# RMS norm with SiLU on one core: VectorE's and ScalarE's code aligned to instruction-fetch blocks

## The chip, the cores and the metric

The kernel runs on 1 core of a Trainium2 chip. The metric is the device time of one execution in microseconds; the kernel before takes 316.89 us (median of 3 runs, 316.89 to 317.03). TensorE is PE in the profile, VectorE DVE, ScalarE ACT, GpSimd POOL and SyncE SP; a small q behind a name means the engine's sequencer, which issues DMAs and waits on semaphores.

## The reference

For an input x of 8 x 1024 rows with 2048 float32 numbers each, a vector gamma of 2048 numbers and eps = 1e-5:

```python
rms = np.sqrt(np.mean(x ** 2, axis=-1, keepdims=True) + eps)
out = gamma * x / rms
return out * (1 / (1 + np.exp(-out)))
```

64 MB are read and 64 MB are written.

## The kernel before

The 8192 rows are cut into 16 blocks of 512 rows. A block has 128 partitions with J = 4 rows each, 4 MB in all. On the chip a ring of BUFS = 6 blocks holds them; block b lies in place b modulo 6. Each block is loaded, worked on in place and stored from the same place, so the load of block b + 6 waits until the store of block b is complete. Blocks 4 and 5 are a pair: each partition holds 8 rows that follow each other in memory, and one transfer loads both (`load_pair`, L69 to L71).

The steps of a block, with their lines:

- `load` (L66, L67): one DMA of 4 MB, issued by ScalarE's queue.
- `squares_scalar` (L78) and `squares_vector` (L86): the sums of squares of the block's four rows, one or two of them on ScalarE and the rest on VectorE, each with its read of the accumulator.
- `root` (L95): ScalarE takes the square root, with a table load ahead of it. `invert` (L100): VectorE takes the reciprocal.
- `multiply` (L105): VectorE multiplies each row by its factor and by g, which is gamma on all partitions.
- `silu` (L113): ScalarE applies Silu, two rows at a time, with a table load ahead of it. `store` (L117): one DMA of 4 MB, issued by SyncE.

The last block takes another way: VectorE multiplies by g alone (L177), and ScalarE's Silu (L179) takes the factor as its scale.

The order of the work is written out by hand under `tc.manual_schedule()`: the instructions of an engine stand in its queue as the code names them. The first ones are what the change touches:

- L121: ScalarE issues the load of block 0.
- L122, L123: VectorE fills `ones` and `eps_t`.
- L124: ScalarE runs one small Square on `ones`, which brings a table load ahead of it.
- L125: SyncE issues the load of gamma (8 KB) into one partition of g. L126 to L128: TensorE multiplies it by a row of ones, so that gamma comes to stand on all partitions of the PSUM tile `junk_v`.
- L129: ScalarE issues the load of block 1.
- L130: VectorE copies `junk_v` to g. L131: ScalarE copies one column of `junk_v`.
- L132 to L135: ScalarE issues the loads of blocks 2 and 3, and of the pair of blocks 4 and 5.

After that comes the loop over the blocks. The load of block 6 stands in ScalarE's queue ahead of the squares of block 3's turn, and the later ones between a block's squares (`loads`) or between the two Silu steps (`between`).

In the built program VectorE has 170 instructions in the kernel's body and ScalarE 145, the waits that stand alone among them.

Of the kernel before, what the change touches and what calls it, by code (L numbers as in the profile page):

```python
# [1 line left out]

# [4 lines left out]

ACT = mybir.ActivationFunctionType
ALU = mybir.AluOpType


@with_exitstack
def kernel(
    ctx: ExitStack,
    tc: tile.TileContext,
    x: bass.AP,
    gamma: bass.AP,
    eps: bass.AP,
    out: bass.AP,
):  # L20

    nc = tc.nc
    P = nc.NUM_PARTITIONS
    f32 = mybir.dt.float32
    x2 = x.flatten_outer_dims()
    o2 = out.flatten_outer_dims()  # L30
    n, d = x2.shape
    J = 4
    BUFS = 6
    nblk = n // (P * J)
    PAIRS = (4,)

    def view(t, b):

        for q in PAIRS:
            if b in (q, q + 1):  # L40
                both = t[q * P * J:(q + 2) * P * J, :].rearrange("(p j) d -> p (j d)", p=P, j=2 * J)
                return both[:, (b - q) * J * d:(b - q + 1) * J * d]
        return t[b * P * J:(b + 1) * P * J, :].rearrange("(p j) d -> p (j d)", p=P, j=J)

    singles = ctx.enter_context(tc.tile_pool(name="singles", bufs=1))
    small = ctx.enter_context(tc.tile_pool(name="small", bufs=2))
    psum = ctx.enter_context(tc.tile_pool(name="psum", bufs=1, space=bass.MemoryType.PSUM))

    Q = 4
    w = d // Q  # L50
    g = singles.tile([P, d], f32)
    eps_t = singles.tile([P, 1], f32)
    ones = singles.tile([P, P], f32)
    junk_a = psum.tile([P, d], f32, name="junk_a")
    junk_v = psum.tile([P, d], f32, name="junk_v")
    ring = singles.tile([P, BUFS * J * d], f32, name="xt")
    sss, rmss, rstds = {}, {}, {}

    def rows(b, j, k):
        at = (b % BUFS) * J + j  # L60
        return ring[:, at * d:(at + k) * d]

    def row(b, j):
        return rows(b, j, 1)

    def load(b):  # L66
        nc.scalar.dma_start(out=rows(b, 0, J), in_=view(x2, b))  # L67

    def load_pair(b):  # L69
        both = x2[b * P * J:(b + 2) * P * J, :].rearrange("(p j) d -> p (j d)", p=P, j=2 * J)  # L70
        nc.scalar.dma_start(out=rows(b, 0, 2 * J), in_=both)  # L71

    def squares_scalar(b, loads=()):


        sss[b] = small.tile([P, J], f32, name="ss")
        for j in range(share(b)):
            nc.scalar.activation(out=junk_a, in_=row(b, j), func=ACT.Square,  # L78
                                 accum_out=sss[b][:, j:j + 1])
            if j == 0:  # L80
                for s in loads:
                    load(s)

    def squares_vector(b):
        for j in range(share(b), J):
            nc.vector.tensor_tensor_reduce(  # L86
                out=junk_v, in0=row(b, j), in1=row(b, j), scale=1.0, scalar=0.0,
                op0=ALU.mult, op1=ALU.add, accum_out=sss[b][:, j:j + 1])

    def share(b):  # L90
        return 1 if 4 <= b <= 12 and b % 2 == 0 else 2

    def root(b):
        rms = small.tile([P, J], f32, name="rms")
        nc.scalar.activation(out=rms, in_=sss.pop(b), func=ACT.Sqrt, scale=1.0 / d, bias=eps_t)  # L95
        rmss[b] = rms

    def invert(b):
        rstd = small.tile([P, J], f32, name="rstd")
        nc.vector.reciprocal(out=rstd, in_=rmss.pop(b))  # L100
        rstds[b] = rstd

    def multiply(b):
        for j in range(J):
            nc.vector.scalar_tensor_tensor(out=row(b, j), in0=row(b, j), scalar=rstds[b][:, j:j + 1],  # L105
                                           in1=g, op0=ALU.mult, op1=ALU.mult)

    def silu(b, between=()):
        for h in range(0, J, 2):
            if h:  # L110
                for s in between:
                    load(s)
            nc.scalar.activation(out=rows(b, h, 2), in_=rows(b, h, 2), func=ACT.Silu)  # L113
        store(b)

    def store(b):
        nc.sync.dma_start(out=view(o2, b), in_=rows(b, 0, J))  # L117

    with tc.manual_schedule():

        load(0)  # L121
        nc.vector.memset(ones, 1.0)  # L122
        nc.vector.memset(eps_t, float(eps))  # L123
        nc.scalar.activation(out=junk_a[:, 0:1], in_=ones[:, 0:1], func=ACT.Square)  # L124
        nc.sync.dma_start(out=g[0:1, :], in_=bass.AP(tensor=gamma.tensor, offset=gamma.offset, ap=[[d, 1], [1, d]]))  # L125
        for c in range(Q):  # L126
            cols = slice(c * w, (c + 1) * w)
            nc.tensor.matmul(junk_v[:, cols], ones[0:1, :], g[0:1, cols], start=True, stop=True)  # L128
        load(1)  # L129
        nc.vector.tensor_copy(out=g, in_=junk_v)  # L130
        nc.scalar.copy(out=junk_a[:, 0:1], in_=junk_v[:, d - 1:d])  # L131
        for b in range(2, PAIRS[0]):  # L132
            load(b)
        for b in PAIRS:
            load_pair(b)  # L135

        last = nblk - 1
        SOON = 3  # L140
        squares_scalar(0)
        squares_vector(0)
        root(0)
        invert(0)
        for b in range(last):
            loads = [b + 3] if BUFS + 2 <= b + 3 < nblk else []
            between = []
            if b + 3 == BUFS:

                load(BUFS)  # L150
                between = [BUFS + 1]
            if b < SOON:
                multiply(b)
                squares_scalar(b + 1, loads)
                silu(b)
                squares_vector(b + 1)
                root(b + 1)
            elif b < last - 1:
                squares_scalar(b + 1, loads)
                squares_vector(b + 1)  # L160
                root(b + 1)
                multiply(b)
                silu(b, between)
            else:
                multiply(b)
                squares_scalar(b + 1)
                silu(b)
                squares_vector(b + 1)
                root(b + 1)
            if b + 1 < last:  # L170
                invert(b + 1)


        for j in range(J):
            if j == J // 2:
                invert(last)
            nc.vector.tensor_mul(out=row(last, j), in0=row(last, j), in1=g)  # L177
        for j in range(J):
            nc.scalar.activation(out=row(last, j), in_=row(last, j), func=ACT.Silu,  # L179
                                 scale=rstds[last][:, j:j + 1])  # L180
        store(last)


# [1 line left out]
_INS = ['x', 'gamma', 'eps']  # L185
_OUTS = [((8, 1024, 2048), 'float32')]

_NUMBERS = {'eps': 9.999999747378752e-06}


# [26 lines left out]
```

## Time and profile before

| What | Value |
| --- | --- |
| median of 3 runs | 316.89 us (316.89 to 317.03) |
| the profiled execution's span, first to last instruction | 315.4 us |
| last instruction of ScalarE's Silu (L179) ends | 291.5 us |
| VectorE busy | 235.2 us |
| ScalarE busy | 212.5 us |
| PE busy | 7.2 us |
| HBM read, written | 67.12 MB, 67.11 MB |
| longest wait in total: VectorE's L86 for loads | 25.9 us in 8 waits |

Times count from the span's start. The page has the busy time of each engine, the span in 40 equal slices (a digit is the busy share in tenths), and the DMA queues: q1 carries the stores and gamma, q10 the loads, q14 instructions. A line of a queue gives packets, MB and the share of 16 DMA engines' time. The DMA view of a window counts the packets that start in it.

The start in order of time, from the timeline:

| Start, us | What |
| --- | --- |
| 0.73 | ScalarE's queue issues the load of block 0, SyncE's that of gamma |
| 0.83 | VectorE, first memset (L122), 0.17 us |
| 1.13 | ScalarE, table load of L124, 1.28 us |
| 1.20 | ScalarE's queue issues the load of block 1 |
| 2.43 | ScalarE, L124 |
| 3.10 | TensorE, first weight load (L128) |
| 10.32 | VectorE, copy of g (L130), 2.29 us |
| 12.71 | ScalarE, L131 |
| 12.73 | ScalarE's queue issues the loads of blocks 2 and 3, at 13.58 that of the pair |
| 13.19 | VectorE, first sum of squares (L86) |
| 35.29 | SyncE's queue issues the first store |

### The profile page before, as it was taken

How to read it: one execution, taken by the hardware profiler on the slowest of the kernel's cores; microseconds unless marked ns; L12 is line 12 of the kernel's file. 1: busy time of each engine (PE TensorE's matmuls, PEld its weight loads, DVE VectorE, ACT ScalarE, POOL GpSimd, SP SyncE). 2: the span in 40 equal slices, each digit the busy share in tenths (PEclk: the TensorE clock that was granted, in tenths of full speed). 3: DMA queues.
4: the chain of work that ended last, by engine and by line, in shares of the span. 5: the costliest groups of instructions: out<-in, count | busy, mean ns of one | idle time of the engine just before them, and what ended most of it. 6: DMA issues, size and time to landing. Idle time of an engine off the chain costs nothing.

```text
span 315.4 us, 436 instructions
## 1 busy us (share of the span) xinstructions
PE 7.2 (2%) x8; PEld 2.5 (1%) x8; DVE 235.2 (75%) x157; ACT 212.5 (67%) x137; POOL 0.2 (0%) x4
## 2 busy tenths in 40 slices
PE   6300000000000000000000000000000000000000
PEld 2000000000000000000000000000000000000000
DVE  0679697944999999999693996939969399994000
ACT  1269998952289968993919849097591999999000
POOL 0000000000000000000000000000000000000000
DMA  8999999999999999999999999999999999999996
GB/s 333 411 453 411 386 532 399 399 440 424 428 437 424 437 432 432 432 432 440 424 440 424 445 420 457 407 457 407 465 399 465 399 465 399 465 403 461 411 453 270
DMA packets 4468, 134.24 MB, mean 426 GB/s; under 512 B 497, under 2 KB 497, under 8 KB 497
## 3 DMA queue, kind: packets, MB, share of 16 engines
q10 hardware_dynamic: 2160, 67.11, 49.6%
q1 hardware_dynamic: 2306, 67.12, 49.3%
q14 instruction: 2, 0.02, 0.0%
HBM read 67.12 MB, written 67.11 MB: 426 GB/s over the span
## 4 chain that ended last, share of the span: by engine, by line
DMA 55%; ACT 18%; DVE 14%; issue 2%; another core or an unknown queue 2%; ACTq 1%; DVEq 0%
DMA out_dram<-xt 40%; DMA xt<-in_x_dram 15%; ACT xt L113 9%; DVE xt L105 9%; DVE junk_v L86 5%; ACT junk_a L78 3%; ACT L95 2%; ACT xt L179 2%; ACT L113 1%; ACTq L212 1%; ACT rms L95 1%; ACTq L67 0%; ACT L179 0%; DVE rstd L100 0%
## 5 line engine op out<-in xcount | busy, mean ns | idle before, releaser
L105 DVE SCALAR_TENSOR_TENSOR xt<-xt,rstd,g 128x2048 f32<-128x2048 f32 x60 | 137.0, 2346 | 0.1
L113 ACT ACTIVATE xt<-xt 128x4096 f32<-128x4096 f32 x30 | 107.3, 3610 | 7.4 <-DVE xt L105 7.3
L86 DVE CUSTOM_DVE_ANT_0 junk_v<-xt 128x2048 f32<-128x2048 f32 x37 | 85.0, 2296 | 26.6 <-DMA xt<-in_x_dram 25.9
L78 ACT ACTIVATE junk_a<-xt 128x2048 f32<-128x2048 f32 x27 | 50.6, 1873 | 34.5 <-DMA out_dram<-xt 22.7
L95 ACT ACT_TABLE_LOAD x15 | 19.2, 1283 | 20.1 <-DMA out_dram<-xt 10.9
L113 ACT ACT_TABLE_LOAD x14 | 18.0, 1283 | 0.2
L100 DVE RECIPROCAL rstd<-rms 128x4 f32<-128x4 f32 x16 | 2.8, 174 | 15.0 <-ACT rms L95 15.0
L130 DVE COPY g<-junk_v 128x2048 f32<-128x2048 f32 x1 | 2.3, 2291 | 9.3 <-PE junk_v L128 9.3
L177 DVE TENSOR_TENSOR xt<-xt,g 128x2048 f32<-128x2048 f32 x4 | 8.9, 2278 | 0.0
L95 ACT ACTIVATE rms<-ss,eps_t 128x4 f32<-128x4 f32 x16 | 4.8, 297 | 5.5 <-DVE ss L86 5.3
L179 ACT ACTIVATE xt<-xt,rstd 128x2048 f32<-128x2048 f32 x4 | 7.7, 1990 | 0.0
L128 PE MATMUL junk_v<-g,ones 1*128 1x512 f32 x8 | 7.2, 1072 | 3.1 <-DMA g<-in_gamma_dram 3.1
L131 ACT COPY junk_a<-junk_v 128x1 f32<-128x1 f32 x1 | 0.1, 144 | 10.1 <-DVE g L130 10.1
L86 DVE DVE_READ_ACCUMULATOR2_ANT ss<- 128x1 f32 x37 | 5.2, 141 | 0.0
L78 ACT ACTIVATION_READ_ACCUMULATOR junk_a<-xt 128x1 f32 x27 | 5.0, 186 | 0.0
L128 PEld LDWEIGHTS junk_v<-g,ones 1*128 1x128 f32 x8 | 2.5, 325 | 6.2 <-issue 6.2
L124 ACT ACT_TABLE_LOAD x1 | 1.3, 1283 | 1.1 <-PEq L198 1.1
L179 ACT ACT_TABLE_LOAD x1 | 1.3, 1283 | 0.0
L122 DVE MEMSET ones<- 128x128 f32 x1 | 0.2, 165 | 0.8 <-PEq L198 0.8
L124 ACT ACTIVATE junk_a<-ones 128x1 f32<-128x1 f32 x1 | 0.2, 174 | 0.0
L198 POOL MEMSET const-bfloat16-1.0<- 128x1 bf16 x1 | 0.1, 103 | 0.0
L198 POOL MEMSET const-uint8-127<- 128x1 uint8 x1 | 0.1, 103 | 0.0
(3 smaller groups left out, 0.3 us busy)
## 6 DMA issues: line engine op xcount, KB each, us to landing
out_dram<-xt SPq DMA_DIRECT2D x16, 4096.0 KB, 39.1
xt<-in_x_dram ACTq DMA_DIRECT2D x14, 4096.0 KB, 26.6
g<-in_gamma_dram SPq DMA_DIRECT2D x1, 8.0 KB
xt<-in_x_dram ACTq DMA_DIRECT2D x1, 61.8
```

Source lines behind the costliest of these rows:

```text
L78: nc.scalar.activation(out=junk_a, in_=row(b, j), func=ACT.Square, accum_out=sss[b][:, j:j + 1])
L86: nc.vector.tensor_tensor_reduce(out=junk_v, in0=row(b, j), in1=row(b, j), scale=1.0, scalar=0.0, op0=ALU.mult, op1=ALU.add, accum_out=sss ...
L95: nc.scalar.activation(out=rms, in_=sss.pop(b), func=ACT.Sqrt, scale=1.0 / d, bias=eps_t)
L100: nc.vector.reciprocal(out=rstd, in_=rmss.pop(b))
L105: nc.vector.scalar_tensor_tensor(out=row(b, j), in0=row(b, j), scalar=rstds[b][:, j:j + 1], in1=g, op0=ALU.mult, op1=ALU.mult)
L113: nc.scalar.activation(out=rows(b, h, 2), in_=rows(b, h, 2), func=ACT.Silu)
L124: nc.scalar.activation(out=junk_a[:, 0:1], in_=ones[:, 0:1], func=ACT.Square)
L128: nc.tensor.matmul(junk_v[:, cols], ones[0:1, :], g[0:1, cols], start=True, stop=True)
L130: nc.vector.tensor_copy(out=g, in_=junk_v)
L177: nc.vector.tensor_mul(out=row(last, j), in0=row(last, j), in1=g)
L179: nc.scalar.activation(out=row(last, j), in_=row(last, j), func=ACT.Silu, scale=rstds[last][:, j:j + 1])
L212: with _tile.TileContext(nc) as tc:
```

## The change

Two lines are added that are no work. `addr_align(FETCH, max_nops=0)` tells the program's loader that the next instruction of this engine begins at a multiple of FETCH instructions (256 in the built program) of the engine's code in memory. The instructions in between are filling; with `max_nops=0` a branch jumps over them, so they are not run. On VectorE the directive stands ahead of its first instruction of the kernel (L122), on ScalarE behind the issue of block 1's load (L129) and ahead of L131. No other instruction is added, removed or moved. Three lines are added in all, so lines behind them have a number higher by 1 to 3 in the kernel after.

```diff
     J = 4
     BUFS = 6
+    FETCH = bass.FETCH_BLOCK_INSTRUCTIONS
     nblk = n // (P * J)
...
         load(0)
+        nc.vector.addr_align(FETCH, max_nops=0)
         nc.vector.memset(ones, 1.0)
         nc.vector.memset(eps_t, float(eps))
         nc.scalar.activation(out=junk_a[:, 0:1], in_=ones[:, 0:1], func=ACT.Square)
...
         load(1)
+        nc.scalar.addr_align(FETCH, max_nops=0)
         nc.vector.tensor_copy(out=g, in_=junk_v)
         nc.scalar.copy(out=junk_a[:, 0:1], in_=junk_v[:, d - 1:d])
```

## The prediction

> **What bounds the kernel now.** I read the page's slices and queue list first, then the chain that ended last, then the DMA view in narrow windows, and last the packet records of the trace one by one.
>
> ```profile
> span 315.4 us, 436 instructions
> DMA  8999999999999999999999999999999999999996
> DMA packets 4468, 134.24 MB, mean 426 GB/s; under 512 B 497, under 2 KB 497, under 8 KB 497
> q10 hardware_dynamic: 2160, 67.11, 49.6%
> q1 hardware_dynamic: 2306, 67.12, 49.3%
> q14 instruction: 2, 0.02, 0.0%
> DMA 55%; ACT 18%; DVE 14%; issue 2%; another core or an unknown queue 2%; ACTq 1%; DVEq 0%
> ```
>
> The DMA row is at nine or more in 38 of 40 slices, while VectorE is busy for 75% of the span and ScalarE for 67%. Loads (q10) and stores (q1) together take 98.9% of what 16 DMA engines have. So the DMA engines set the time. An engine of computation that is some us late costs nothing as long as transfers stay queued. The third queue line is the one that this change can touch: two packets that carry instructions.
>
> The windows of the DMA view tell when they run.
>
> ```profile
> DMA packets 15, 0.47 MB, mean 778 GB/s; under 512 B 0, under 2 KB 0, under 8 KB 0
> q14 instruction: 1, 0.01, 3.2%
> ```
>
> That is 92.5 to 93.1 us; the window from 106.4 to 107 us shows the other one:
>
> ```profile
> DMA packets 7, 0.11 MB, mean 178 GB/s; under 512 B 3, under 2 KB 3, under 8 KB 3
> q14 instruction: 1, 0.01, 3.2%
> ```
>
> Both lie where the DMA engines are full. The packet records give start, duration, bytes and queue, but no DMA engine. I joined each packet to the one that starts within some ns of its end. This gives 16 chains, one for each DMA engine, and each holds 240 packets of 32 KB at 1.213 us and 8 of 64 KB. No chain has a gap above 0.05 us between 2.9 us and its end: all 16 are never idle. Fifteen chains end between 312.91 and 313.39 us, and one at 314.28 us. The window from 313.39 to 314.29 us holds only that chain's last, small packet:
>
> ```profile
> DMA packets 1, 0.00 MB, mean 0 GB/s; under 512 B 1, under 2 KB 1, under 8 KB 1
> ```
>
> The last store is complete when the slowest DMA engine is, so this one chain sets the end by 0.89 us. It is the chain that carries the instruction packet of 106.49 us. There the instruction packet took 0.309 us and the 32 KB packet after it 1.747 us in place of 1.213: 0.309 + 0.534 = 0.84 us. The packet of 92.71 us, on another chain, took 0.309 us and its successor 1.333: 0.309 + 0.120 = 0.43 us; that chain ends at 313.39. Without its fetch the late chain would end at 314.28 - 0.84 = 313.44, beside the others.
>
> Who fetches is not recorded. The packets start 1.05 and 1.11 us after VectorE starts a sum of squares (91.66 and 105.38 us), and ScalarE starts a Silu at 91.69 us. By then the built program stands at about the 50th to the 60th instruction on each of the two. So I take it that VectorE and ScalarE each cross an edge of their code there, one packet of 8 KB each.
>
> **The change, part by part.** It adds one directive on each of the two engines and removes nothing. The built programs show nothing moved: the same order of work on every engine, with 170 instructions and one directive on VectorE, 145 and one on ScalarE. The directive's alignment is 256 instructions, so either engine's remaining code is shorter than one aligned block.
>
> *VectorE's branch, ahead of the memset of L122.* The trace shows no branch of this kind. Its cost lies between a semaphore instruction (17 to 28 ns) and a fetch from memory, for which the nearest row is gamma's 8 KB load: issued at 0.73 us, used by TensorE at 3.13 us, so 2.4 us. Behind the branch stands the memset (0.83 us). For it wait ScalarE's L124 with the second load issue (1.20 us) behind it, and TensorE's weight load (3.10 us, beside gamma's landing). At 2.4 us the memset ends at about 3.4 us, TensorE is 0.3 us late, and so are the copy of g (10.32 us) and the issues of loads 2 to 5 (12.73 us). These must be in the queue before loads 0 and 1 are through: the second load ends at 22.77 us, and the first load's packets start up to 2.2 us after their issue. So 22.77 - 2.2 - 12.73 = 7.8 us are free. The second load itself, at 3.6 us instead of 1.2, is due by about 1.64 + 8 x 1.21 - 2.2 = 9.1 us. Cost: nothing, for anything between the two ends. Its packet falls at about 1 us, before the first data packet (1.64 us): nothing again.
>
> *ScalarE's branch, behind the second load issue.* Behind it stand L131 and the loads from 12.73 us on. ScalarE waits 10.1 us before L131 for the copy of g anyway, so a stall of 2.4 us plus two packets ahead of it (2 x 1.21) is hidden. Its fetch, however, starts at about 1.6 us plus a latency like the 1.05 us above, when the chains are just filling: first packets start between 1.64 and 2.88 us and take up to 2.39 us. One DMA engine pays between nothing (if the packet slips in ahead of that engine's first data) and 0.84 us, the dearest of the two above. I take 0.43, the nearer row, as part of it falls into the ragged start. Fifteen of the chains, without fetches, would end at 312.91 to 313.39, mean 313.17; 313.17 + 0.43 = 313.60, and 313.44 is the floor that the once late chain sets.
>
> *What goes away.* Neither engine crosses an edge in the full stretch, so 0.84 and 0.43 us leave two chains. Late next is the chain of the new ScalarE fetch, at 313.44 to 313.9, likeliest 313.6 to 313.7.
>
> **Sum.** 313.64 - 314.28 = -0.64 us. The profiled span is 315.43 us and the median of the runs 316.89, which is 1.46 us above; I keep that distance. 316.89 - 0.64 = **316.25 us**, 0.20% below. A difference of 0.2% (0.63 us) is about what a measurement of this kernel can tell from no change, and the forecast lies on that line.
>
> The Trainium skill ("Runtime: NRT & Kernel Launch", Instruction fetch mechanics) says that crossing a block edge costs one bump of a queue's tail and is mostly hidden. For the two engines' own time this agrees: no idle time of theirs is charged to a fetch. By that rule nothing would be won and the time would stay at 316.89, which is the fourth case below. The trace speaks against it at the DMA engines: 0.84 us on the one chain that ends last.
>
> **The rivals.**
>
> *More fetches than before, stacked on one DMA engine (slower).* A jump leaves the sequence of the code, so its target may have to be fetched, and the block behind it too. Two fetches of ScalarE on one DMA engine at the start, when all are filling, cost 2 x 0.43 to 2 x 0.84. On the chain with the least slack that ends at 313.44 + 0.86 = 314.30 to 313.44 + 1.69 = 315.13, so 316.9 to 317.7 us. It decides once two packets share a DMA engine that has less than 0.84 us of slack. For it: the gap of 13.8 us between the two packets of before lets each belong to one engine, so engines may have a DMA engine of their own. Against: the part behind the branch may be in the engine already.
>
> The same section of the Trainium skill warns that a taken branch out of the two fetched blocks must wait for a transfer. No row here shows such a branch.
>
> *The edges come back.* If the edge that counts lies every 128 instructions (8 KB, what one instruction packet carries: the built program gives 64 bytes for an instruction), both engines cross another one behind their 128th instruction, where the DMA engines are full. Two chains then pay 0.43 to 0.84 us again and end at 313.39 to 314.28: 316.0 to 316.9 us, middle 316.6. For it: the packets are 8 KB, half of 256 instructions. Against: the code that lies behind may be fetched already.
>
> *The fetch is hidden or does not go away.* The directive is without effect on the two packets, or the late chain is late for another reason (its first packet, 2.387 us, was the slowest too, though 313.44 accounts for that): 316.9 us.
>
> *The queue runs dry.* A stall above 7.8 us at the start leaves the DMA engines without work, and each us beyond costs one: 317.5 us and above. Against: a DMA engine alternates between queues after one or two packets, as the chains show, so a fetch waits some 2.4 us.
>
> **How the numbers follow.** Forecast 0.47 (0.35 faster, 0.12 within 0.2%); more fetches 0.20 (0.05 within, 0.15 slower); edges come back 0.23 (0.05 faster, 0.16 within, 0.02 slower); hidden or without effect 0.06 (within); dry 0.04 (slower). Together: faster 0.40, within 0.39, slower 0.21. The range reaches from 316.0 (all of 0.84 us gone, a little lower if the start falls better: 315.95) to most of the stacked fetches, 317.5. Faster and slower cases both count; the forecast's own range is 316.0 to 316.55.
>
> **What would show it.** Right: no q14 packet between 5 us and the end; the last packet within 0.3 us of the second last chain; first memset up to 2.4 us later than 0.83; TensorE, the copy of g and the load issues at most 1 us later; still no gap in a chain. Wrong: q14 packets behind 100 us; more than two of them, or of 16 KB; a chain that stands alone at the end by over 0.5 us; a gap in the chains at about 22 us; and a changed duration of the 32 KB packets, which I hold to stay at 1.213 us.

## The result, and the profile after

The kernel after takes 318.18 us (median of 5 runs, 317.84 to 318.35) against 316.89 us (316.79 to 317.18): a ratio of 1.0037, with a 95% interval of 1.0024 to 1.0049. It is 1.3 us slower, where 0.64 us faster was forecast, and lies above the range.

The page of the kernel after, in the same order as that of before:

```profile
span 316.2 us, 438 instructions
DMA  8999999999999999999999999999999999999995
DMA packets 4472, 134.28 MB, mean 425 GB/s; under 512 B 497, under 2 KB 497, under 8 KB 497
q10 hardware_dynamic: 2160, 67.11, 49.6%
q1 hardware_dynamic: 2306, 67.12, 49.2%
q14 instruction: 6, 0.05, 0.0%
DMA 54%; ACT 18%; DVE 14%; issue 3%; another core or an unknown queue 2%; ACTq 1%; DVEq 0%
```

Loads and stores are what they were, packet for packet. The one count that moved is q14: six packets of 8 KB in place of two, and 134.28 MB in place of 134.24. The share "0.0%" hides them, since it is a mean over 16 DMA engines.

The DMA view in three narrow windows: 1.5 to 2.2, 7.7 to 8.0 and 216 to 216.6 us.

```profile
q14 instruction: 1, 0.01, 6.8%
...
q14 instruction: 1, 0.01, 6.9%
...
q14 instruction: 1, 0.01, 3.2%
```

The packet records, joined to 16 chains as in the prediction, give these for the two chains that end last. "Next" is the 32 KB packet behind the instruction packet on the same DMA engine; without a fetch it takes 1.213 us.

| Chain | Instruction packets: start (duration, next), us | End, us |
| --- | --- | --- |
| before, ScalarE's | 92.71 (0.309, 1.333) | 313.39 |
| before, VectorE's | 106.49 (0.309, 1.747) | 314.28 |
| after, ScalarE's | 8.48 (0.309, 1.598), 14.03 (0.309, 1.594), 229.39 (0.309, 1.333) | 314.54 |
| after, VectorE's | 1.80 (0.759, 1.628), 7.81 (0.329, 1.876), 216.33 (0.309, 1.569) | 315.02 |

The other 14 chains of the kernel after end between 313.02 and 314.10 us. The last chain ends 315.02 - 314.28 = 0.74 us later than before, and the span is 316.19 - 315.43 = 0.75 us longer: that is all of the span's difference. Which chain belongs to which engine is shown by the first two experiments.

The start of VectorE in the timeline of the kernel after (start, duration, engine, line; in brackets the idle time before it):

```profile
4.01 0.17 DVE L124 MEMSET ones<- 128x128 f32 x1 [4.01 <-issue]
```

The same line of the kernel before:

```profile
0.83 0.17 DVE L122 MEMSET ones<- 128x128 f32 x1 [0.83 <-PEq L198]
```

Nothing that the profile shows held VectorE for the 3.2 us in between ("issue"). In the trace the branch runs at 0.75 us and the first instruction packet is in flight from 1.80 to 2.56 us, so I read the wait as one for the code behind the jump; the experiments bear that out.

The medians differ by 1.29 us, the profiled spans by 0.75. In nine of the ten profiled runs from here on, this one among them, the time is 1.78 to 1.79 us above the span (the tenth is told below), 317.97 - 316.19 = 1.78 in the kernel after. By that the profiled execution of before took about 315.43 + 1.79 = 317.2 us, 0.3 above its median, and not 1.46 above the span. The profiled run of after, 317.97, lies 0.2 below its own median.

### The profile page after: what moved, and what is told of

Its sections match the earlier page's. It is cut to its first block, busy times and chain, and to the rows that moved or that the text cites. A ratio compares the mean times of both kernels' runs of the same rounds, so it can differ in the third digit from the quotient of the medians.

```text
span 316.2 us, 438 instructions
## 1 busy us (share of the span) xinstructions
PE 7.2 (2%) x8; PEld 2.5 (1%) x8; DVE 235.2 (74%) x157; ACT 212.5 (67%) x137; POOL 0.2 (0%) x4
## 2 busy tenths in 40 slices
DMA packets 4472, 134.28 MB, mean 425 GB/s; under 512 B 497, under 2 KB 497, under 8 KB 497
## 4 chain that ended last, share of the span: by engine, by line
DMA 54%; ACT 18%; DVE 14%; issue 3%; another core or an unknown queue 2%; ACTq 1%; DVEq 0%
DMA out_dram<-xt 40%; DMA xt<-in_x_dram 15%; ACT xt L114 9%; DVE xt L106 9%; DVE junk_v L87 5%; ACT junk_a L79 3%; ACT L96 2%; ACT xt L182 2%; ACT L114 1%; ACTq L215 1%; ACT rms L96 1%; ACT L182 0%; ACTq L68 0%; DVE rstd L101 0%
```

## Experiments

Theory of fetches: the loss is the added instruction packets, which stand one behind the other on the DMA engine of each issuing engine, and the slowest DMA engine sets the end. Rival: the loss is the 3.2 us of VectorE's stall, which puts all work behind it about 1.1 us later. Each time stands against runs of the kernel before on the same chip. An edit is shown against the kernel after where nothing else is said.

### VectorE's directive alone

```diff
-        nc.scalar.addr_align(FETCH, max_nops=0)
```

> Only VectorE's directive. Theory of fetches: the loss comes from more instruction packets on two DMA engines (6 in the kernel after, 2 in the one before). Here VectorE keeps its stall (first memset at 4.0 us), and 4 packets are expected: two of the start and one of the two late ones (216 or 229 us) are VectorE's, one of before (92.7 or 106.5 us) stays ScalarE's. The worst chain ends at 314.3 to 314.8 us, the time is 316.9 to 317.5 us. Rival theory of the late start: all of the loss comes from the work behind VectorE's first memset being 1.1 us later, so the time is that of the kernel after, 318.2 us.

318.25 us, ratio 1.0036 (1.0023 to 1.0049). From the page's list of queues:

```profile
q14 instruction: 4, 0.03, 0.0%
```

Three packets come much as in the kernel after, at 1.93, 7.82 and 216.67 us, and one more at 96.44. So the group of 1.8, 7.8 and 216 us is VectorE's, all on one DMA engine, and 92.7 us before was ScalarE's. Where two chains run within a few ns of each other the join by times alone has two ways. Each load or store of blocks, however, gives every chain eight data packets and then one of 4 bytes. With that order kept, VectorE's three packets lie on the chain that ends last, at 315.64 us. On that chain several single packets between 151 and 264 us are late as well, by some 0.5 us together; why is open. By the medians VectorE's directive alone has the whole loss, though its seven runs spread from 317.65 to 319.13 us. The forecast of 316.9 to 317.5 was too low: I had given VectorE's DMA engine too little for three packets. On time alone this run speaks for either theory.

### ScalarE's directive alone

```diff
-        nc.vector.addr_align(FETCH, max_nops=0)
```

> Only ScalarE's directive. Theory of fetches: the first memset stays at 0.83 us, 4 packets in the span, two of them between 2 and 15 us and one late; worst chain 314.3 to 314.8 us, time 316.9 to 317.5 us. Rival theory of the late start: nothing of VectorE's or TensorE's start is later, so the time is that before, 316.9 us.

317.61 us, ratio 1.0023 (1.0014 to 1.0031). The first memset is at 0.82 us, and the page has 4 instruction packets: 6.43 (next 1.459), 11.84 (1.593) and 229.79 us (1.333) are ScalarE's, 107.41 VectorE's; with the order of the packets kept as above, all three lie on the chain that ends last. ScalarE's three cost 3 x 0.309 + 0.246 + 0.380 + 0.120 = 1.67 us; that chain ends at 314.93 us and the other 15 at 312.94 to 314.41. Nothing starts late here, and there is a loss: the rival does not hold for it. This loss (0.7 us) and that of VectorE's directive (1.3) do not add up to that of both (1.3). The loss of both is the larger one, as it should be where the slowest of 16 DMA engines sets the end.

### The late start without a jump

```diff
+        nc.vector.memset(junk_v, 0.0)
+        nc.vector.memset(junk_v[:, 0:d // 2], 0.0)
         nc.vector.memset(ones, 1.0)
```

(against the kernel before)

> No directive; VectorE fills PSUM for about 3.3 us ahead of its first memset (two fills of junk_v, which TensorE overwrites), so that the memset comes at about 4.1 us as in the kernel after, with no jump. Theory of fetches: two packets near 93 and 106 us as before, time 316.9 us within 0.3. Rival theory of the late start: 318.2 us.

317.01 us, ratio 1.0002 (0.9993 to 1.001). From its timeline:

```profile
4.21 0.17 DVE L124 MEMSET ones<- 128x128 f32 x1
...
4.42 0.33 ACTq L67 DMA_DIRECT2D xt<-in_x_dram  x1
...
14.07 0.82 ACTq L67 DMA_DIRECT2D xt<-in_x_dram  x2
```

The memset, the second load and the loads behind it are as late as in the kernel after (4.01, 4.21 and 13.87 us there) or later, and the time does not move. There are two instruction packets, at 93.96 and 106.11 us. The rival falls: the DMA queue covers the late start, as the prediction's margin of 7.8 us said.

### The filling run as no-operations

```diff
-        nc.vector.addr_align(FETCH, max_nops=0)
+        nc.vector.addr_align(FETCH, max_nops=255)
...
-        nc.scalar.addr_align(FETCH, max_nops=0)
+        nc.scalar.addr_align(FETCH, max_nops=255)
```

> Both directives, but with the filling run as no-operations in sequence and no branch over it (up to 255 of them). Theory of fetches, if the jump out of the sequence makes the start's packets: fewer packets before 20 us than the 4 of the kernel after, the two late ones near 216 and 229 us stay; time 316.9 to 317.6 us. If the aligned edge itself makes them: 6 packets and 318.2 us. Rival theory of the late start: the time follows the delay of the first memset, whatever the packets are.

321.15 us, ratio 1.0133 (1.012 to 1.0146). Six packets again, at 7.57, 13.27, 18.00, 23.41, 221.71 and 232.36 us: it is not the jump that makes them, but the edges passed. The trace also tells where the code stands, for it records 189 no-operations on VectorE and 185 on ScalarE. Without the filling the next instruction would thus stand 189 and 185 places ahead of a multiple of 256, that is at places 67 and 71 when they are counted from the multiple before. On either engine the filling passes two multiples of 128 but only one of 256, and two packets came. The time, though, has another cause. From the timeline:

```profile
10.47 0.17 DVE L124 MEMSET ones<- 128x128 f32 x1 [10.47 <-issue]
...
10.67 0.33 ACTq L68 DMA_DIRECT2D xt<-in_x_dram  x1
```

The second load is issued at 10.67 us, when the first is nearly through. The windows view from 11.5 to 15 us (length; busy time of each engine; the last three columns are the clock, the DMA share and GB/s):

```profile
11.50:15.00 3.50, 3.50 (x5) 1.33 (x4) 0.00 (x0) 0.00 (x0) 0.00 (x0) 1.00 0.85 293
```

In the kernel after the same window has 1.04 and 442 GB/s. The chains have gaps of up to 2.1 us here: the queue runs dry, which was the last of the prediction's rivals. Neither of the two theories had reckoned with it, so the time tells nothing between them.

### Aligned to 128

```diff
-    FETCH = bass.FETCH_BLOCK_INSTRUCTIONS
+    FETCH = bass.FETCH_BLOCK_INSTRUCTIONS // 2
```

> Both directives, aligned to 128 instructions instead of 256. Theory of an edge every 128 instructions, with one 8 KB packet for each edge that an engine passes, on a DMA engine of its own: the jump passes one edge in place of two, to a block that is in the engine already. So no stall of VectorE (first memset at 0.83 us), 4 packets in the span (one of each engine before 15 us, one of each near 216 and 229 us). Worst chain 314.1 to 314.8 us, time 316.8 to 317.4 us. If the edge lies every 256 instructions: 6 packets or 2, a stall, and 318.2 us or the time before.

317.62 us, ratio 1.0019 (1.001 to 1.0028). From the timeline, and then from the page's queues:

```profile
1.37 0.17 DVE L124 MEMSET ones<- 128x128 f32 x1 [1.37 <-PEq L201]
```

```profile
q14 instruction: 4, 0.03, 0.0%
```

Four packets: 4.07 and 216.08 us on one chain, which ends last at 314.77, 6.06 and 228.91 us on the other. One packet of each engine fewer, and the stall of 3.2 us is down to half a us. So an edge lies every 128 instructions, each edge passed makes one packet, and a jump over one edge finds its target there, while a jump over two has to wait for it. The time is 0.2 us above what I expected, the packets are as expected.

### A jump that passes no edge

```diff
+    FETCH = bass.FETCH_BLOCK_INSTRUCTIONS // 2
...
+        nc.vector.addr_align(FETCH, offset=80, max_nops=0)
...
+        nc.scalar.addr_align(FETCH, offset=80, max_nops=0)
```

(against the kernel before)

> Both directives with the same branch over filling, but to the place 80 behind an edge of 128 instructions, so that by the places found so far no edge is passed by the jump. Theory of edges: 2 packets in the span as in the kernel before, one of each engine, earlier than 92 and 106 us as the code stands some 20 places further on (near 55 to 80 us); no stall; time 316.9 us within 0.5. Rival theory that the branch itself costs, or makes a fetch: 4 packets or more, and a time above 317.4 us.

317.29 us, ratio 1.0008 (0.9999 to 1.0017). Two packets in the span, at 79.53 and 86.82 us, and the first memset at 1.02 us: the jump itself costs 0.2 us of VectorE's time, which is hidden. The profiled span is 314.9 us and the last chain of data ends at 313.76 us; the median span of all eleven runs, 315.0 us, is about that of the kernel before on this chip, 315.1. The time is longer by 0.4 us because the part behind the span is: 317.11 - 314.91 = 2.21 us in place of 1.79. The DMA view from 314 to 318 us:

```profile
DMA packets 2, 0.02 MB, mean 4 GB/s; under 512 B 0, under 2 KB 0, under 8 KB 0
...
q14 instruction: 2, 0.02, 1.3%
```

Two more instruction packets start behind the kernel's last instruction, at 316.69 and 316.96 us. With VectorE's code 80 behind an edge its 170 instructions end at place 250, close to the edge at 256. That these packets make the 0.42 us is likely, but no run here tells it apart.

### ScalarE's jump twice

```diff
+    FETCH = bass.FETCH_BLOCK_INSTRUCTIONS
...
         load(1)
+        nc.scalar.addr_align(FETCH, max_nops=0)
...
             load_pair(b)
+        nc.scalar.addr_align(FETCH, max_nops=0)
```

(against the kernel before)

> ScalarE's directive twice: behind the second load issue as in the kernel after, and once more behind the pair's load issue; none on VectorE. Theory of edges: two more packets than with ScalarE's directive alone (6 in the span, 5 on ScalarE's DMA engine), at 0.55 to 0.84 us each, so the chain that ends last at 314.9 us there ends at 316.0 to 316.6 us, and the time is 318.7 to 319.3 us against the 317.6 us with one. Rival theory that only the start or the late packets count: 317.6 us.

320.06 us, ratio 1.0094 (1.0078 to 1.0109). Six packets, five of them on one chain: 6.34, 11.74, 18.49, 24.03 and 232.05 us. That chain ends last, at 317.18 us, 1.75 us behind the next. The count is as expected, the time 0.8 us above the expected 318.7 to 319.3. The rest is not fetches. The two added packets and their neighbours cost 2 x 0.309 + 0.381 + 0.379 = 1.38 us of the 2.25 us by which the last chain ends later than with one jump (314.93 us). A single 32 KB packet at 87.2 us, 0.84 us longer than usual, makes up nearly all that remains. It is not alone: between 74 and 92 us packets of the other 15 chains are longer by 1.1 to 2.0 us together, where the kernel before lost nothing, and these chains end at 314.2 to 315.4 in place of about 313.2. Ahead of that, ScalarE's second jump stalls it while the DMA engines are full, as the timeline shows (this run, then the kernel before):

```profile
20.20 1.88 ACT L79 ACTIVATE junk_a<-xt 128x2048 f32<-128x2048 f32 x1 [7.54 <-issue]
...
14.13 1.88 ACT L78 ACTIVATE junk_a<-xt 128x2048 f32<-128x2048 f32 x1 [1.28 <-issue]
```

The idle time ahead of this Square grew from 1.28 to 7.54 us, so the jump held ScalarE for 6.3 us, twice VectorE's stall at the empty start. The load of block 6 is issued at 72.05 us in place of 66.83. The slow packets follow this delay, but that it causes them is not shown. About two fifths of the 2.4 us over one jump are thus of another kind than fetches.

### VectorE at places 72 and 68

```diff
+    FETCH = bass.FETCH_BLOCK_INSTRUCTIONS // 2
...
+        nc.vector.addr_align(FETCH, offset=72, max_nops=0)
```

(against the kernel before; the other has offset=68)

> Only VectorE's directive, to the place 72 behind an edge of 128 instructions: some 8 places further on than in the kernel before. Theory of edges: 2 packets in the span; VectorE's comes near 90 to 97 us in place of 106 us, ScalarE's stays near 93 us; the time is 316.9 us within 0.4, the sign by whether the 32 KB packet behind VectorE's instruction packet is a load (up to 0.53 us longer) or a store (0.12 to 0.36 us longer). The end part behind the span, which was 0.42 us longer with both engines at place 80 (2.21 against 1.79 us), stays at 1.79 us if it was a further edge in the code behind the kernel's body. Rival theory that the branch itself costs: above 317.3 us.

> As with place 72, but place 68: VectorE's packet near 97 to 103 us; 2 packets in the span, 316.9 us within 0.4, end part behind the span 1.79 us. Rival theory that the branch itself costs: above 317.3 us, the same as with place 72.

Place 72: 316.96 us, ratio 1.0002 (0.9993 to 1.001). Place 68: 316.95 us, ratio 1.0004 (0.9995 to 1.0013). Two packets in either, and the part behind the span is 1.79 us in both: a directive on VectorE whose jump passes no edge costs nothing that can be measured. The packet's time was missed. VectorE's came at 81.96 us with place 72 and at 106.22 with 68, about where the kernel before has it, in place of 90 to 97 and 97 to 103. I had taken the code to stand near place 64; the no-operations counted above put it at 67, so the two runs moved it by five places and by one, not by eight and four. One place fits a packet at the old time. Why five places bring it 24 us earlier is not settled. These were tried as versions that could beat the kernel before. None does.

## Why the prediction was wrong

Point by point:

- *What bounds the kernel.* Right. Loads and stores kept their packets, the chains stayed full in every run but the one with no-operations (the prediction overlooked a gap of 0.25 us on one chain of the kernel before, at 38 us; most runs have one or two such gaps between 38 and 41 us, up to 0.37 us long), and in the kernel after the last chain accounts for 0.74 of 0.75 us of the span.
- *The price of an instruction packet.* About right for the late packets. Apart from VectorE's very first one, a packet cost 0.31 to 0.33 us and its neighbour 0.11 to 0.66 us more, where 0.12 and 0.53 were read from before. ScalarE's packet of the start, put at 0.43 us, cost 0.69 and came twice.
- *The stalls cost nothing.* Right, by the late start without a jump. The stall, 3.2 us, was longer than the 2.4 us taken from gamma's load, and TensorE's first weight load moved by 1.1 us, not 0.3; both inside the margin. The Trainium skill ("Runtime: NRT & Kernel Launch", Instruction fetch mechanics) has a taken branch out of the fetched blocks wait for a transfer; the stalls of 3.2 and 6.3 us agree, but the first was hidden: the kernel after did not lose its time by it.
- *VectorE's packet falls before the first data packet: nothing again.* Wrong. It started at 1.80 us, with the first data packet at 1.65 us, and the stack on that DMA engine had begun.
- *What goes away.* This is the step that failed: "Neither engine crosses an edge in the full stretch, so 0.84 and 0.43 us leave two chains." The code was shorter than 256 instructions, and I let the directive's 256 stand for the edge. The edge lies every 128 instructions. So both engines pass one again, at 216 and 229 us, and each jump to a multiple of 256 passes two, so that two packets of each engine came at the start where the sum had one. With 170 instructions VectorE passes at least one edge wherever its code begins: its packet could be moved, but not removed. The 8 KB of a packet, half of 256 instructions, had pointed to this in the profile of before, and the prediction used it for a rival only.
- *The rivals.* Two of them came true together: more fetches on one DMA engine, and the edges come back. I priced each alone, as if one excluded the other. On VectorE's chain 0.329 + 0.663 at 7.81 us and 0.309 + 0.356 at 216.33 make 1.66 us, and the packet at 1.80 us some 0.33 more (its chain is through with the first load packet at 4.18 us, the others at 3.85 on average): 2.0 us on a chain that would have ended at 313.0. Before, that chain carried 0.84.
- *The distance from span to time.* 1.46 us was a median less the span of one profiled execution that was itself slower than the median. The runs here give 1.79. So the chain that I read as typically 0.89 us late was likely less so in a median run, and less could be won than one profile showed.

The rule of the Trainium skill that a block edge is mostly hidden (same section) was weighed in the prediction. For the engines' own time it holds in the kernel before, where no idle time of theirs is charged to an edge passed in sequence. For the DMA engines it does not: apart from VectorE's very first one, a packet and the delay of its neighbour took 0.42 to 1.0 us, and they were the loss.

## What to carry to other kernels

Where the DMA engines are full from end to end, the time is that of the slowest of them, and packets that no share shows (0.05 MB of 134) set it: join the packets to chains and look at who ends last. Count the instruction packets of a code layout by the edges that it passes, jumps over filling included, before moving code to an edge: aligning to 256 added two edges at the start for each engine and took none away. When two rivals can both be true, give their sum a case of its own.

## What the runs showed of the hardware

- Instruction packets of VectorE all go to one DMA engine, and those of ScalarE to another (three and three in the kernel after, five of ScalarE's with its jump twice). One packet of 8 KB comes for each edge of 128 instructions that is passed, by a jump or in sequence (6 packets either way).
- A jump over two edges held VectorE for 3.2 us at an empty start, and ScalarE for 6.3 us with full DMA engines; a jump over one edge held VectorE for 0.5 us, a jump over none for 0.2 us.
- A 32 KB packet behind an instruction packet took 1.33 to 1.88 us in place of 1.213.
- Around 36 to 42 us, where the first store joins the loads, every DMA engine loses time (0.5 to 0.8 us in the kernel before), and single packets are slower still, on changing DMA engines: up to 2.81 us for 32 KB in the kernel after, 2.94 us with VectorE's directive alone. In the late start without a jump such a packet (2.67 us), not a fetch, makes the last chain. Why is open; it may be part of the spread between runs.
